# Moving loads between queues and skipping a round trip through memory in a fused retention / state-space layer on Trainium2

## The chip, the cores and the metric

The kernel runs on one NeuronCore of a Trainium2 chip. A core has five engines, each with an instruction queue that is worked off in order: TensorE (PE, matrix products), VectorE (DVE), ScalarE (ACT), GpSimd (POOL) and SyncE (SP, which only starts transfers). DMA transfers are started by an instruction on SP's, ACT's or POOL's queue. The metric is device time in microseconds (us); lower is better. Before the change the median of three runs is 2652.86 us (2648.1 to 2653.33).

## What is computed

One layer of a hybrid decoder in float32, on 1024 prompt tokens and 8 sample tokens (1032 columns, width 2048), with the same weights for both:

```python
def layer(x, pos, s_ret, s_re, s_im, ...):
    h = rmsnorm(x, g_pre)
    proj = h @ w_in                                   # 2048 x 10240
    q, k, v, za, ub, zb, ga, gb = jnp.split(proj, splits, axis=-1)
    ya, s_ret_new = retention(q, k, v, pos, s_ret)    # 8 heads, chunks of 128, normalized per head
    ya = (ya * jax.nn.silu(za)) @ w_pa
    yb, s_re_new, s_im_new = s5(ub, ...)              # ends in gelu and y * sigmoid(y @ w_glu + b_glu)
    yb = (yb * jax.nn.silu(zb)) @ w_pb
    merged = jax.nn.sigmoid(ga) * ya + jax.nn.sigmoid(gb) * yb
    out = merged @ w_out
    return x + rmsnorm(out, g_post), s_ret_new, s_re_new, s_im_new
```

## The kernel before

**Layout and products.** Tokens lie along the free axis, 1032 = 2 x 516 columns (`TOK` = 2 `HT`); features lie on the 128 partitions, so a 1024-wide activation is eight tiles. Each float32 product is three TensorE products of a high and a low part. `split` (L255) makes the two parts of a token tile: ACT casts a copy to the high part (L256) and DVE subtracts it from the source (L84, the line of every DVE addition, subtraction and product). Weights are split in the same way: L202 for plain products and L873 for the Strassen products.

**Stages, in order.** First `ub` and the S5 scan with the steps of `w_in`; retention runs as background work in the second half of `w_in` (about 1350 to 1822 us); then the gated linear unit of S5 (GLU, `linear(I["w_glu"], ...)`, 8 output tiles by 2 halves by 3 thirds of the tokens, to about 1913 us); then eight steps of `pa`, the first gated projection (`ya @ w_pa`), and eight of `pb` (`yb @ w_pb`) to about 2272 us; then `merged @ w_out` in two parts, first the rest of the tokens (392 columns), then the other 640.

**Strassen steps.** `w_in`, `pa` and `pb` go through 2 x 2 blocks of weights and token halves by a seven-product form. For one step, `fetch(s + 1)` starts the four weight loads (SP), `prep(g + 2)` makes weights two products ahead (DVE additions, ACT cast `whi`, DVE `wlo`), `product(g)` (L880) issues 48 plus 48 matmuls, and `evac_p` takes the result out of the accumulators; three accumulators rotate. The token operands are seven forms of the halves: u1 and v1 (halves of features 0 to 3 and 4 to 7), v2, and the four sums t1, t3, t2, t4 that `make_forms` builds. They sit in SBUF as split pairs found by `qslot("pa", n, i)` for product n and feature tile i; `order_q` is the list of the 28 pairs in the order of use.

**The GLU's background.** While the GLU's products run, `glu_forms` makes the forms of `pa`. `make_forms` loads the eight `ya_d` tiles into `fx` (POOL's queue), DVE builds the sums in place, and both halves of each form go to memory (`fa_d`). Then `stage` (L835) loads one half tile after another into eight `stg` buffers, 24 of the 28 within the GLU, and `unstage` splits them. The GLU's evacuation (`evac_glu`) is ACT's sigmoid (L1379), a DVE product, a store and the load of the next gate `zz<-zy_d`. Ahead of the GLU all left-over late work of the last `w_in` step is issued in one piece: `due` holds functions by product number (`at(g, f)`), `late_work(g)` issues them. In that last step they are the accumulation of partial sums (`u<-pt_d`), ACT's sigmoid on them (L972) and their stores to `sgb_d`.

**Gates and merging.** `load_z` (L1442) loads a gate half (`zz<-sga_d` in `pa`, `zz<-sgb_d` in `pb`) by POOL's queue. `gated` multiplies an evacuated result tile by it. In `pa` the product goes to `pap_d`. In `pb`, POOL adds `pap_d` onto the tile by an accumulating transfer (L1464), and four products later (`LAG`) stores the sum to `mg_d` (L1465). In the last step the second token half is added to a loaded `pap_d` half by DVE instead (L1445, L1460). `mg_load` (L1502) loads the 392 columns of merged tokens for the output stage by POOL, `mg_split` splits them (ACT, DVE).

**Retention.** `head(h)` is a generator; each `yield` is a step of background work given to the scheduler after a product. At its end come the normalization's statistics (DVE), the power -1/2 on POOL (L1135, L1136), `rsd` times a column and `nb` (DVE, L1137 to L1139), a `yield`, nine normalizations on ACT (L1142, L1143), a `yield`, and transposes on TensorE (L1149).

**What sets the order.** Background generators are advanced by `slot()` once a product. A scheduler then orders instructions by priority, and every engine's queue stays in that order.

Of the kernel before, what the change touches and what calls it, by code (L numbers as in the profile page):

```python
# [10 lines left out]
F32 = mybir.dt.float32  # L11
# [16 lines left out]
TA = 640  # L28
# [50 lines left out]
def emit(ctx, tc, I, O):  # L79
# [9 lines left out]
    def add(out, a, b, eng=None):  # L89
        return tt(out, a, b, ALU.add, eng)  # L90
# [164 lines left out]
    def split(dst, src):  # L255
        A.copy(dst[0], src)  # L256
        sub(dst[1], src, dst[0].bitcast(F32))
# [542 lines left out]
    def popen(name, side, bufs):  # L800
        st = ExitStack()
        return st, st.enter_context(tc.tile_pool(name=name, bufs=bufs, side=side))
# [14 lines left out]
    def qslot(kh, n, i):  # L817
        j = (2 * n + i // 2 + {0: 0, 1: -2, "pa": 4, "pb": 2}[kh]) % 16
        grp = 0 if kh in (0, 1) else kh
        if (grp, j) not in qtile:  # L820
            qtile[grp, j] = act.tile([128, 2, 2, HT], F32R, name=f"a{j}")
        return qtile[grp, j][:, i % 2, 0, :], qtile[grp, j][:, i % 2, 1, :]
# [3 lines left out]
    def stage(pool, kh, n, i, eng=P):  # L826
        r = stq[kh, n, i] = pool.tile([128, HT], F32, name="stg")
        if kh in (0, 1):
            src = fm_d[kh, n, i]
        else:  # L830
            y, F = (ya_d, fa_d) if kh == "pa" else (yb_d, fb_d)
            f = FORMS[n]
            src = {"u1": y[i], "v1": y[4 + i], "v2": y[4 + i], "t1": F[0, i], "t3": F[0, i], "t4": F[1, i], "t2": F[1, i]}[f]
            src = src[:, 0:HT] if f in ("u1", "v1", "t1", "t4") else src[:, HT:TOK]
        eng.dma_start(r, src)  # L835

    def unstage(kh, n, i):
        split(qslot(kh, n, i), stq.pop((kh, n, i)))
# [69 lines left out]
    def at(g, f):  # L908
        due.setdefault(g, []).append(f)
# [122 lines left out]
    def head(h):  # L1032
# [101 lines left out]
        V.tensor_scalar(rs[0:8, 8:9], mv[0:8, 8, 1:2], EPS, None, ALU.add)  # L1134
        P.tensor_tensor(rs[:, 0:8], rs[:, 0:8], mhalf, ALU.pow)  # L1135
        P.tensor_tensor(rs[0:8, 8:9], rs[0:8, 8:9], mhalf[0:8, 0:1], ALU.pow)  # L1136
        V.tensor_scalar(rs[:, 0:8], rs[:, 0:8], col[:, 2, h:h + 1], None, ALU.mult)  # L1137
        V.scalar_tensor_tensor(nb[:, 0:8], mv[:, 0:8, 0], -1.0, rs[:, 0:8], ALU.mult, ALU.mult)
        V.scalar_tensor_tensor(nb[0:8, 8:9], mv[0:8, 8, 0:1], -1.0, rs[0:8, 8:9], ALU.mult, ALU.mult)  # L1139
        yield  # L1140
        for n in range(8):
            A.activation(on[:, n], on[:, n], AF.Identity, scale=rs[:, n:n + 1], bias=nb[:, n:n + 1])  # L1142
        A.activation(ons, ons, AF.Identity, scale=rs[0:8, 8:9], bias=nb[0:8, 8:9])  # L1143
# [90 lines left out]
    def late_work(g):  # L1234
        with ExitStack() as after:
            for ins in anchor.values():
                after.enter_context(tc.issue_after(ins))
            for f in due.pop(g, ()):
                f()
# [4 lines left out]
    for s in range(2 * NP):  # L1244
# [41 lines left out]
        for n in range(7):  # L1286
# [26 lines left out]
                        at(g, lambda m=m: load_gy(6 + m))  # L1313
            late_work(g)
            slot()
    for g in sorted(due):
        late_work(g)
    gstack.close()


    bglu = const.tile([128, 8], F32, name="bglu")
# [9 lines left out]

    def stg_open(bufs):
        opened["stg"], opened["stgp"] = popen("stg3", "left", bufs)

    def make_forms(src, F):

        t = {}

        def ld(i):
            t[i] = [opened["fxp"].tile([128, TOK], F32, name="fx") for _ in range(2)]  # L1340
            for x, k in zip(t[i], (i, 4 + i)):
                P.dma_start(x, src[k])

        ld(0)
        ld(1)
        for _ in range(3):
            yield
        for i in range(4):
            u, v = t.pop(i)
            u1, u2, v1, v2 = u[:, 0:HT], u[:, HT:TOK], v[:, 0:HT], v[:, HT:TOK]  # L1350
            sub(u1, u1, u2)
            sub(u2, u2, v2)
            yield
            add(v2, v2, u1)
            sub(v1, v1, v2)
            P.dma_start(F[0, i], u)
            P.dma_start(F[1, i], v)
            yield
            if i < 2:
                yield  # L1360
                yield
                ld(i + 2)
                yield
        opened["fx"].close()
# [17 lines left out]
            load_zy(3 * m + t + 4)  # L1382
        return f

    def glu_forms():
        yield from make_forms(ya_d, fa_d)
        stg_open(8)
        for o in order_q[0:8]:
            stage(opened["stgp"], "pa", *o)
        for _ in range(3):  # L1390
            yield
        for z in range(16):
            unstage("pa", *order_q[z])
            stage(opened["stgp"], "pa", *order_q[z + 8])
            yield

    def tail_forms():
# [10 lines left out]
    for k in range(4):  # L1408
        load_zy(k)
    fx_open()  # L1410
    bg.append(glu_forms())
    S0 = 2 * NP
    lim[0] = 7 * len(steps)

# [23 lines left out]
    def load_z(s, name):  # L1438
        kind, p = steps[s]
        r, c = AT[name]  # L1440
        zq[name] = zz_tile()
        P.dma_start(zq[name], (sga_d if kind == "pa" else sgb_d)[2 * p + r, :, HT * c:HT * c + HT])  # L1442
        if s == len(steps) - 1 and c:
            zq[name, "p"] = zz_tile()
            P.dma_start(zq[name, "p"], pap_d[2 * p + r, :, HT * c:HT * c + HT])  # L1445

    def gated(g, name, t, ps=None):
        s = g // 7
        kind, p = steps[s]
        r, c = AT[name]  # L1450
        m, cols = 2 * p + r, slice(HT * c, HT * c + HT)
        z = zq.pop(name)
        if ps is None:
            mul(t, t, z)
        else:
            mul(two(t), ps, two(z))
        if kind == "pa":
            P.dma_start(pap_d[m, :, cols], t)
        elif (name, "p") in zq:
            add(t, t, zq.pop((name, "p")))  # L1460
            last_t[m] = t
            P.dma_start(mg_d[m, :, HT:TA], t[:, 0:TA - HT])
        else:
            P.dma_start(t, pap_d[m, :, cols], accum_op=ALU.add)  # L1464
            at(g + LAG, lambda: P.dma_start(mg_d[m, :, cols], t))  # L1465

    def evac_p(g, ps):
        n = g % 7
# [30 lines left out]

    def mg_load(m):  # L1500
        mgr[m] = mgp.tile([128, SW], F32, name="mga")
        P.dma_start(mgr[m], mg_d[m, :, TA:TOK])  # L1502

    def mg_split(m, src=None):
        mg_open(m)
        split((mg[m][0][:, TA:TOK], mg[m][1][:, TA:TOK]), mgr.pop(m) if src is None else src)
# [4 lines left out]
    for s in range(S0, len(steps)):  # L1511
        kind, p = steps[s]
        if s == S0 + 1:
            opened["stg"].close()
            fx_open()
            bg.append(make_forms(yb_d, fb_d))
        if s == S0 + 6:
            drain()
            stg_open(8)
        if s == S0 + 9:  # L1520
            opened["stg"].close()
            mgstack, mgp = popen("mgp", "left", 6)
        for n in range(7):
            g = 7 * s + n
            if n == 1:
                fetch(s + 1)
            prep(g + 2)
            evac_p(g, product(g))
            if n in (0, 2, 3, 4):
                at(g, lambda s=s, n=n: load_z(s, {0: "11", 2: "22", 3: "21", 4: "12"}[n]))  # L1530
            if s == S0 and n < 6:
                for _ in range((2, 1, 1, 1, 2, 1)[n]):
                    at(g, lambda o=order_q[pa_q[0]]: unstage("pa", *o))
                    if pa_q[0] + 8 < 28:
                        at(g, lambda o=order_q[pa_q[0] + 8]: stage(opened["stgp"], "pa", *o))
                    pa_q[0] += 1
            q = g - 7 * (S0 + 6)
            if 0 <= q < 4:
                for _ in range(2):
                    at(g, lambda o=order_q[nxt]: stage(opened["stgp"], "pb", *o))  # L1540
                    nxt += 1
            if 3 <= q < 20:
                for i in range(1 if q < 7 else 2):
                    if done_q < 28:
                        at(g, lambda o=order_q[done_q]: unstage("pb", *o))
                        done_q += 1
                        if nxt < 28:
                            at(g, lambda o=order_q[nxt]: stage(opened["stgp"], "pb", *o))
                            nxt += 1
            if s == SE - 1 and n in (1, 2, 3):  # L1550
                for m in (2 * n - 2, 2 * n - 1):
                    at(g, lambda m=m: mg_load(m))
            if s == SE - 1 and n in (5, 6):
                at(g, lambda m=n - 5: mg_split(m))
            if s == SE and n < 6:
                for m in (2 + 2 * n, 3 + 2 * n) if n < 5 else (13,):
                    at(g, lambda m=m: mg_split(m))
                for m in (6 + 2 * n, 7 + 2 * n) if n < 3 else ((13,) if n == 3 else (12,) if n == 4 else ()):
                    at(g, lambda m=m: mg_load(m))
            late_work(g)  # L1560
            slot()
    for m in (12, 15, 14):
        mg_split(m, last_t[m][:, TA - HT:HT] if m in last_t else None)
    for g in sorted(due):
        late_work(g)
    mgstack.close()
# [265 lines left out]
```

## Time and profile before

| what | before |
|---|---|
| median of the runs | 2652.86 us (2648.1 to 2653.33, 3 runs) |
| the profiled execution | 2650.8 us |
| its span | 2648.8 us |
| mean granted TensorE clock | 0.993 |
| gate loads `zz` from `sga_d`, `sgb_d` by POOL | 32 and 32, of 258 KB |
| loads of merged tokens `mga` by POOL | 14, of 196 KB |
| `ya_d` loads into `fx` | 8, of 516 KB |

An instruction row of the trace gives its start, its length, the engine (PEld is a weight load, POOLq a queue), the line, the operation, output and inputs, the size and, in brackets, how long the engine was idle before and what released it. In a wait row the numbers are the total, the count and the longest of the waits. Matmuls are pipelined and their ends are modelled.

Six windows of the span divide it by stage. The columns are window, length, busy time of PE, PEld, DVE, ACT and POOL (with counts), granted clock, DMA share, GB/s.

```profile
0.00:230.00 230.00, 224.53 (x1414) 222.24 (x1415) 135.94 (x204) 70.24 (x97) 28.66 (x67) 1.00 0.76 242
230.00:1350.00 1120.00, 1119.01 (x9277) 1111.62 (x9276) 918.91 (x2213) 377.91 (x667) 312.34 (x528) 1.00 0.54 152
1350.00:1822.00 472.00, 467.60 (x3955) 462.10 (x3954) 305.50 (x664) 212.52 (x395) 189.25 (x278) 1.00 0.79 215
1822.00:1913.00 91.00, 80.09 (x491) 79.35 (x490) 40.37 (x69) 28.45 (x52) 43.37 (x81) 0.94 0.89 300
1913.00:2272.00 359.00, 341.82 (x2780) 340.82 (x2779) 247.50 (x395) 109.60 (x191) 134.33 (x228) 0.98 0.74 221
2272.00:2648.00 376.00, 365.00 (x1744) 321.44 (x1744) 190.53 (x312) 154.74 (x278) 56.61 (x88) 0.99 0.61 194
```

TensorE is idle for about 11 us in the GLU and 17 us in `pa` and `pb`; the fourth and fifth rows are those stages. In the last row TensorE's last matmul begins at 2637.3 us.

### The profile page before, as it was taken

The numbers are of one execution on the slowest core, as the hardware profiler recorded it, in microseconds if no ns is written. First come the engines' busy times: TensorE is split into PE (matmuls) and PEld (weight loads), VectorE is DVE, ScalarE is ACT, GpSimd is POOL, SyncE is SP. The second block draws the span as 40 slices with busy tenths as digits, with TensorE's granted clock in tenths as the row PEclk, the third lists the DMA queues.
The fourth block names the chain that finished last, engine by engine and source line by source line (L and its number), as shares of the span: only waits on it lengthen the run. The fifth ranks groups of instructions, "written<-read, shape, count | busy, mean of one in ns | idle before, by whom it ended". The sixth has DMA issues, their size and how long they took to land. (4 is left out here: it accounts for less than half of the span.)

```text
span 2648.8 us, 51289 instructions
## 1 busy us (share of the span) xinstructions
PE 2598.1 (98%) x19652; PEld 2537.6 (96%) x19652; DVE 1838.8 (69%) x3853; ACT 953.5 (36%) x1679; POOL 764.6 (29%) x1268
## 2 busy tenths in 40 slices
PE   9999999999999999999999999999899999899998
PEld 8999999999999999999999999999899999898886
DVE  6655989889889867558877666665477865444555
ACT  6013233323333335442244444444332422343344
POOL 0103322222222223322244433333533434211111
PEclk9999999999999999999999999999999999899999
DMA  5886444443443457876688777779876767745666
GB/s 189 270 263 206 147 122 123 131 130 120 120 139 121 121 170 218 215 199 166 160 229 238 206 199 216 193 181 292 290 246 237 241 183 191 221 163 173 195 194 231
DMA packets 225525, 506.60 MB, mean 191 GB/s; under 512 B 32720, under 2 KB 53664, under 8 KB 225152
## 3 DMA queue, kind: packets, MB, share of 16 engines
q0 software_dynamic: 102672, 301.07, 40.5%
q1 hardware_dynamic: 103072, 179.57, 21.5%
q10 hardware_dynamic: 19536, 22.69, 2.8%
q8 instruction: 154, 2.52, 0.4%
q14 instruction: 91, 0.75, 0.1%
HBM read 345.20 MB, written 158.01 MB: 190 GB/s over the span
## 5 line engine op out<-in xcount | busy, mean ns | idle before, releaser
L892 PE MATMUL acc<-a,whi 128*128 128x258 f32 x9632 | 1565.7, 284 | 19.5 <-DVE u L84 16.1
L892 PEld LDWEIGHTS acc<-a,whi 128*128 128x128 f32 x9632 | 1328.4, 190 | 26.2 <-ACT whi L873 13.3
L892 PE MATMUL acc<-a,wlo 128*128 128x258 f32 x4816 | 970.4, 283 | 0.0
L892 PEld LDWEIGHTS acc<-a,wlo 128*128 128x128 f32 x4816 | 746.3, 190 | 0.0
L84 DVE TENSOR_TENSOR wlo<-wraw,whi 128x512 fp32r<-128x512 f32 x482 | 330.9, 687 | 238.7 <-ACT whi L202 141.9
L873 ACT CAST whi<-wraw 128x512 fp32r<-128x512 f32 x344 | 213.4, 620 | 617.5 <-PE acc L892 516.5
L873 ACT CAST whi<-wr 128x512 fp32r<-128x512 f32 x258 | 160.0, 620 | 517.8 <-PE acc L892 477.2
L209 PE MATMUL mm<-a,whi 128*128 128x384 f32 (+2 forms) x704 | 233.7, 333 | 8.3 <-ACT whi L202 5.4
L210 PE MATMUL mm<-a,whi 128*128 128x384 f32 (+2 forms) x704 | 233.5, 332 | 0.0
L211 PE MATMUL mm<-a,wlo 128*128 128x384 f32 (+2 forms) x704 | 232.3, 330 | 0.1
L84 DVE TENSOR_TENSOR wlo<-wr,whi 128x512 fp32r<-128x512 f32 x273 | 187.0, 685 | 53.1 <-ACT whi L873 43.0
L1730 PE MATMUL mm<-whi,a 128*128 128x512 f32 x512 | 171.1, 395 | 0.0
L202 ACT CAST whi<-wraw 128x512 fp32r<-128x512 f32 x138 | 85.5, 620 | 208.1 <-PE mm L210 104.6
L209 PEld LDWEIGHTS mm<-a,whi 128*128 128x128 f32 x704 | 133.0, 189 | 8.8 <-ACT whi L202 5.4
L211 PEld LDWEIGHTS mm<-a,wlo 128*128 128x128 f32 x704 | 133.7, 190 | 0.8 <-DVE wlo L84 0.6
L210 PEld LDWEIGHTS mm<-a,whi 128*128 128x128 f32 x704 | 133.5, 190 | 0.6 <-DVE a L363 0.6
L84 DVE TENSOR_TENSOR wraw<-wr 128x512 f32<-128x512 f32 x172 | 118.1, 687 | 5.9 <-DMA wr<-in_w_pa 3.7
L1730 PEld LDWEIGHTS mm<-whi,a 128*128 128x128 f32 x512 | 96.1, 188 | 22.8
L84 DVE TENSOR_TENSOR p<-acc,p 128x516 f32<-128x516 f32 x86 | 59.6, 693 | 72.9 <-PE acc L892 72.7
L84 DVE TENSOR_TENSOR wlo<-wx,whi 128x512 fp32r<-128x512 f32 x76 | 52.5, 691 | 76.0 <-ACT whi L202 75.7
L1730 PE MATMUL mm<-wlo,a 128*128 128x512 f32 x256 | 101.4, 396 | 0.0
L84 DVE TENSOR_TENSOR u<-acc,u 128x516 f32<-128x516 f32 x86 | 59.6, 693 | 59.9 <-PE acc L892 58.7
(369 smaller groups left out, 3483.7 us busy)
## 6 DMA issues: line engine op xcount, KB each, us to landing
wr<-in_w_in SPq DMA_DIRECT2D x280, 256.0 KB
pt_d<-u POOLq DMA_DIRECT2D x70, 258.0 KB, 3.1
u<-pt_d POOLq DMA_DIRECT2D x70, 258.0 KB, 5.3
wraw<-in_w_outB SPq DMA_DIRECT2D x66, 256.0 KB
stg<-fm_d POOLq DMA_DIRECT2D x44, 258.0 KB, 4.3
wx<-in_w_outB SPq DMA_DIRECT2D x43, 256.0 KB
wraw<-in_w_out SPq DMA_DIRECT2D x39, 256.0 KB
pt_d<-st POOLq DMA_DIRECT2D x35, 258.0 KB, 3.1
```

The lines of the kernel that those rows point to most:

```text
L84: return (eng or V).tensor_tensor(out, a, b, op)
L202: anchor["a"] = A.copy(hi, raw).ins
L209: T.matmul(ps, wh[:, i, :], xh[:, t0:t1], start=first, stop=False)
L210: T.matmul(ps, wh[:, i, :], xl[:, t0:t1], start=False, stop=False)
L211: anchor["p"] = T.matmul(ps, wl[:, i, :], xh[:, t0:t1], start=False, stop=last).ins
L873: anchor["a"] = A.copy(hi, f).ins
L892: anchor["p"] = T.matmul(ps[:, j, 0:258], a[:, i, :], b[:, 258 * j:258 * j + 258], start=first and i == 0 and a is wh and b is xh, stop=n ...
L1730: anchor["p"] = T.matmul(ps[c], a, b, start=k == 0 and a is xh and b is wh, stop=k == KD - 1 and a is xl).ins
```

## The change

The change has five parts.

1. In `head`, the `yield` moves up, so that DVE reads POOL's power one background step later.
2. The left-over late work of the last `w_in` step becomes a generator, `left_over`, that `both` advances together with `glu_forms` during the GLU.
3. The new `glu_forms` loads pairs of `ya_d` tiles into `fx` and splits the forms of products 0 to 3 straight from SBUF: u1, t2, v1 and t3. Only the halves t1 and t4 are stored to `fa_d`, and eight half tiles are staged for the rest of the GLU. That leaves out 16 staged loads and half of the stored bytes.
4. Gate loads, the two `pap_d` half loads of the last step and the merged-token loads are started by ACT's queue instead of POOL's.
5. In the last `pb` step, the addition of product "22" goes from DVE to POOL, the merged tokens 12 and 13 are split from the tiles that hold them in SBUF (two loads fewer), and 15 comes ahead of 14.

```diff
@@ head
         P.tensor_tensor(rs[0:8, 8:9], rs[0:8, 8:9], mhalf[0:8, 0:1], ALU.pow)
+        yield
         V.tensor_scalar(rs[:, 0:8], rs[:, 0:8], col[:, 2, h:h + 1], None, ALU.mult)
         V.scalar_tensor_tensor(nb[:, 0:8], mv[:, 0:8, 0], -1.0, rs[:, 0:8], ALU.mult, ALU.mult)
         V.scalar_tensor_tensor(nb[0:8, 8:9], mv[0:8, 8, 0:1], -1.0, rs[0:8, 8:9], ALU.mult, ALU.mult)
-        yield
@@ the end of the w_in steps
-    for g in sorted(due):
-        late_work(g)
     gstack.close()
+    def left_over():
+        for n in range(2, 8):
+            yield
+            for g in sorted(due):
+                if g - 14 * NP <= n - (n > 4) - 2:
+                    late_work(g)
@@ new
+    def glu_forms():
...
+        ld(0)
+        ld(1)
+        for _ in range(6):
+            yield
+        for i in range(4):
+            u, v = t.pop(i)
+            u1, u2, v1, v2 = u[:, 0:HT], u[:, HT:TOK], v[:, 0:HT], v[:, HT:TOK]
+            split(qslot("pa", 0, i), u1)
+            sub(u1, u1, u2)
+            yield
+            split(qslot("pa", 2, i), v1)
+            sub(u2, u2, v2)
+            yield
+            add(v2, v2, u1)
+            P.dma_start(fa_d[0, i, :, 0:HT], u1)
+            split(qslot("pa", 1, i), v2)
+            yield
+            sub(v1, v1, v2)
+            P.dma_start(fa_d[1, i, :, 0:HT], v1)
+            split(qslot("pa", 3, i), u2)
+            yield
+            if i < 2:
+                yield
+                yield
+                ld(i + 2)
+            yield
+        opened["fx"].close()
+        stg_open(8)
+        for o in order_q[16:24]:
+            stage(opened["stgp"], "pa", *o)
@@ load_z
-        P.dma_start(zq[name], (sga_d if kind == "pa" else sgb_d)[2 * p + r, :, HT * c:HT * c + HT])
+        A.dma_start(zq[name], (sga_d if kind == "pa" else sgb_d)[2 * p + r, :, HT * c:HT * c + HT])
...
-            P.dma_start(zq[name, "p"], pap_d[2 * p + r, :, HT * c:HT * c + HT])
+            A.dma_start(zq[name, "p"], pap_d[2 * p + r, :, HT * c:HT * c + HT])
@@ gated
-            add(t, t, zq.pop((name, "p")))
+            add(t, t, zq.pop((name, "p")), P if name == "22" else V)
...
+            if s == len(steps) - 2 and c:
+                last_t[m] = t
@@ mg_load
-        P.dma_start(mgr[m], mg_d[m, :, TA:TOK])
+        A.dma_start(mgr[m], mg_d[m, :, TA:TOK])
@@ the last pb step
-                for m in (2 + 2 * n, 3 + 2 * n) if n < 5 else (13,):
-                    at(g, lambda m=m: mg_split(m))
-                for m in (6 + 2 * n, 7 + 2 * n) if n < 3 else ((13,) if n == 3 else (12,) if n == 4 else ()):
+                for m in (2 + 2 * n, 3 + 2 * n):
+                    at(g, lambda m=m: mg_split(m, last_t[m][:, TA - HT:HT] if m in last_t else None))
+                for m in (6 + 2 * n, 7 + 2 * n) if n < 3 else ():
                     at(g, lambda m=m: mg_load(m))
```

How the instructions stand now is seen on three queues. First DVE at the end of one retention head, as a difference (- before, + now; `u` and `p` are evacuated result tiles, `wraw`, `wlo` weights):

```order
 L1134 TENSOR_SCALAR rsd<-mv 8x1
-L1137 TENSOR_SCALAR rsd<-rsd,col 128x8
-L1139 SCALAR_TENSOR_TENSOR nb<-mv,rsd 8x1
-L1138 SCALAR_TENSOR_TENSOR nb<-mv,rsd 128x8
 L84 TENSOR_TENSOR u_22229<-p_22164,acc 128x516
 L84 TENSOR_TENSOR wlo<-wraw,whi 128x512
-L84 TENSOR_TENSOR wraw<-wraw,wr 128x512
-L84 TENSOR_TENSOR wlo<-wr,whi 128x512
+L1138 TENSOR_SCALAR rsd<-rsd,col 128x8
+L1140 SCALAR_TENSOR_TENSOR nb<-mv,rsd 8x1
+L84 TENSOR_TENSOR wraw<-wraw,wr 128x512
+L1139 SCALAR_TENSOR_TENSOR nb<-mv,rsd 128x8
```

The evacuation `u` and one `wlo` now stand ahead of the reads of POOL's result, and the weight addition `wraw` stands between them and the large `nb`.

Then POOL's queue at the turn from `w_in` to the GLU. Before:

```order
L946 DMA p_22735<-pt_d 128x516
L973 DMA sgb_d<-u_22845 128x516
L1342 DMA fx<-ya_d 128x1032
L946 DMA u_22771<-pt_d 128x516
L973 DMA sgb_d<-p_22735 128x516
L1342 DMA fx<-ya_d 128x1032 x2
L973 DMA sgb_d<-u_22771 128x516
L1342 DMA fx<-ya_d 128x1032
```

The same place now (`pt_d` loads accumulate partial sums, `sgb_d` stores hold the gate):

```order
L946 DMA p_22735<-pt_d 128x516
L1346 DMA fx<-ya_d 128x1032 x2
L946 DMA u_22771<-pt_d 128x516
L1346 DMA fx<-ya_d 128x1032 x2
L973 DMA sgb_d<-u_22845 128x516
L973 DMA sgb_d<-p_22735 128x516
L973 DMA sgb_d<-u_22771 128x516
```

All four `fx` loads of the first two pairs moved ahead of the three `sgb_d` stores.

Last, POOL's queue through the second-to-last step of `pb`; middle steps read the same without the `mga` rows. Before:

```order
L1464 DMA u_27707<-pap_d 128x516
L1502 DMA mga<-mg_d 128x392
L1442 DMA zz<-sgb_d 128x516
L1465 DMA mg_d<-u_27707 128x516
L1464 DMA p_27591<-pap_d 128x516
L1502 DMA mga<-mg_d 128x392
L1445 DMA zz<-pap_d 128x516
L1464 DMA u_27634<-pap_d 128x516
L1502 DMA mga<-mg_d 128x392
L1465 DMA mg_d<-p_27591 128x516
L1442 DMA zz<-sgb_d 128x516
L1465 DMA mg_d<-u_27634 128x516
```

The same place now:

```order
L1511 DMA st<-pap_d 128x516
L1512 DMA mg_d<-st 128x516
L1511 DMA u_27675<-pap_d 128x516
L1512 DMA mg_d<-u_27675 128x516
L1511 DMA p_27559<-pap_d 128x516
L1511 DMA u_27602<-pap_d 128x516
L1512 DMA mg_d<-p_27559 128x516
L1512 DMA mg_d<-u_27602 128x516
```

The accumulating loads and their stores are left; the gate and merged-token loads are on ACT's queue.

More of the change, by code (lines that the diff above doesn't have):

```diff
@@ L1333, in stg_open, with ld @@
         opened["stg"], opened["stgp"] = popen("stg3", "left", bufs)
+    def glu_forms():
+        t = {}
+        def ld(i):
+            t[i] = [opened["fxp"].tile([128, TOK], F32, name="fx") for _ in range(2)]
+            for x, k in zip(t[i], (i, 4 + i)):
+                P.dma_start(x, ya_d[k])
+        ld(0)
[28 more added lines that the diff above has]
+            stage(opened["stgp"], "pa", *o)
     def make_forms(src, F):
@@ L1383, in evac_glu, with both @@
         return f
[L1385 to L1394, printed above, removed]
+    def both():
+        a, b = left_over(), glu_forms()
+        n = 0
+        while True:
+            live = False
+            for x in (a, b):
+                try:
+                    next(x)
+                    live = True
+                except StopIteration:
+                    pass
+            if not live:
+                return
             yield
@@ L1410, in emit @@
     fx_open()
-    bg.append(glu_forms())
+    bg.append(both())
     S0 = 2 * NP
@@ L1561, in emit @@
             slot()
-    for m in (12, 15, 14):
-        mg_split(m, last_t[m][:, TA - HT:HT] if m in last_t else None)
+    for m in (15, 14):
+        mg_split(m, last_t[m][:, TA - HT:HT])
     for g in sorted(due):
```

## The prediction

> **What bounds the kernel now.** I began with the page's busy times and then asked for the waits of TensorE alone.
>
> ```profile
> PE 2598.1 (98%) x19652; PEld 2537.6 (96%) x19652; DVE 1838.8 (69%) x3853; ACT 953.5 (36%) x1679; POOL 764.6 (29%) x1268
> ...
> PE acc L892 <- DVE u L84: 16.1, 12, 11.4
> PE acc L209 <- ACT p L1379: 10.2, 2, 9.2
> ...
> PE mm L209 <- DVE u L84: 2.9, 1, 2.9
> PE acc L892 <- ACT p L1471: 2.7, 1, 2.7
> ```
>
> TensorE is busy for 98% of the span and no matmul is added or removed, so the change can win only what TensorE loses. The waits (total, count, longest) are few: 10.2 us in the GLU, 2.7 us and one 0.73 us in the middle of `pb`, 11.4 and 2.9 us at its end, and eight short ones in retention. The second loss is the granted clock, which falls after each long stall. The windows below begin where TensorE restarts (columns: length, busy of PE, PEld, DVE, ACT, POOL, granted clock, DMA share, GB/s).
>
> ```profile
> 2198.60:2203.60 5.00, 4.81 (x28) 4.81 (x29) 4.09 (x7) 1.10 (x3) 0.35 (x1) 0.66 0.68 165
> 2261.20:2267.20 6.00, 6.00 (x29) 6.00 (x30) 3.77 (x7) 1.98 (x4) 2.60 (x5) 0.53 0.98 252
> 2272.60:2277.60 5.00, 4.95 (x19) 4.98 (x20) 3.36 (x6) 1.04 (x2) 1.10 (x2) 0.66 0.85 223
> 1879.20:1884.70 5.50, 5.44 (x17) 5.44 (x18) 5.50 (x11) 4.49 (x10) 4.27 (x8) 0.51 1.02 388
> ```
>
> Length times the missing clock is lost: 5.0 x 0.34 = 1.7, 6.0 x 0.47 = 2.8, 1.7 and 5.5 x 0.49 = 2.7 us. With these, the GLU stalls cost 10.2 + 2.7 = 12.9, the middle of `pb` 2.70 + 0.73 + 1.7 = 5.1, its end 11.4 + 2.9 + 2.8 + 1.7 = 18.8.
>
> **The GLU (parts 2 and 3).** The chain behind the long stall:
>
> ```profile
> 1871.97 2.12 POOL L835 DMA_DIRECT2D stg<-ya_d  x4 [0.95 <-DMA fa_d<-fx]
> ...
> 1876.84 1.89 ACT L256 CAST a<-stg 128x516 fp32r<-128x516 f32 x3 [12.83 <-DMA stg<-ya_d]
> ...
> 1878.63 0.57 ACT L1379 ACTIVATE p<-acc,bglu 128x384 f32<-128x384 f32 x1
> 1879.26 0.69 PE L209 MATMUL acc<-a,whi 128*128 128x384 f32 x1 [9.22 <-ACT p L1379]
> ```
>
> ACT sat 12.83 us in front of the cast of a staged tile; POOL had issued that load behind the last store of a form. The sigmoid, which frees TensorE's accumulator, is queued behind the casts. In the new order the casts read `fx`, and no staged load stands before a sigmoid until the last eight loads. On POOL the first two `fx` pairs now stand ahead of the last three `sgb_d` stores (the order shown above), where before single `fx` loads stood behind them. DVE and ACT do as many operations as before (16 splits, 16 form operations), and 16 loads and 8 x 258 KB of stores go away in a stretch where the DMA engines are 1.02 busy. What is late next is the first split, or the activation of a late tile in front of the first sigmoid; the second wait of the 10.2 us is of that kind:
>
> ```profile
> 1834.93 0.44 PE L209 MATMUL acc<-a,whi 128*128 128x384 f32 x1 [1.03 <-ACT p L1379]
> ...
> fx<-ya_d POOLq DMA_DIRECT2D x8, 516.0 KB, 6.6
> ```
>
> The `fx` loads take 6.6 us to land and the third and fourth pairs are issued only after two forms are done. Bounds: nothing left, or one landing of 6.6 us and the 2.7 us of slow clock left. I am near the lower end, since two pairs are loaded ahead: about 0.9 us remains, the size of the 1.03 wait. Term: -12.0 (-12.9 to -3.6).
>
> **The middle of `pb` (part 4).** The order of POOL's queue shown above (middle steps read alike without `mga`) explains these rows:
>
> ```profile
> 2182.25 0.70 DVE L84 TENSOR_TENSOR st<-acc,zz 128x516 f32<-128x516 f32 x1 [4.10 <-DMA zz<-sgb_d]
> ...
> 2194.75 0.56 POOL L1465 DMA_DIRECT2D mg_d<-p  x1 [4.80 <-DMA p<-pap_d]
> 2195.30 0.57 POOL L1442 DMA_DIRECT2D zz<-sgb_d  x1
> 2195.32 0.70 DVE L84 TENSOR_TENSOR p<-p,zz 128x516 f32<-128x516 f32 x1 [5.64 <-DMA zz<-sgb_d]
> ...
> 2198.15 0.59 ACT L1471 COPY p<-acc 128x516 f32<-128x516 f32 x1 [4.52 <-DMA mg_d<-p]
> ...
> 2184.30 0.73 PE L892 MATMUL acc<-a,whi 128*128 128x258 f32 x4 [0.73 <-DVE u L84]
> ...
> 2198.79 1.23 PE L892 MATMUL acc<-a,whi 128*128 128x258 f32 x4 [2.70 <-ACT p L1471]
> ```
>
> POOL waits in order for each accumulating transfer before it may store the sum, and the next gate load stands behind that wait: 4.80 us here. DVE then waits 5.64 us for a gate, the result tile is stored late, and ACT's copy into that tile 4.52 us later still, which TensorE sees as 2.70 us. On ACT's queue a gate load passes none of those waits. POOL's own chain is shorter by four issues a step, of 0.57 us in the row above. Both stalls should go: -5.1 (-5.1 to 0).
>
> The issues cost ACT time:
>
> ```profile
> 506.54 1.21 ACTq L715 DMA_DIRECT2D y_d<-a  x2
> ...
> 2187.23 0.62 ACT L873 CAST whi<-wraw 128x512 fp32r<-128x512 f32 x1 [3.25 <-PE acc L892]
> ```
>
> One issue holds ACT for 1.21 / 2 = 0.6 us. 78 of them are 47 us, 64 of them the gates of the 16 steps of `pa` and `pb`: 2.4 us a step. They hide in ACT's idle time: a weight cast here waits 3.25 us for TensorE to free its buffer. Cost 0, or 47 us if nothing hid them. I take 0, because the 3.25 of idle is five times an issue.
>
> The trace has no gate load on ACT's queue, only POOL's landing (`zz<-sgb_d`, 5.3 us in the row quoted with the rivals). The Trainium skill speaks against this part: the page "DMA: Bandwidth & Descriptors", section "Issuing engines are not separate DMA queues", says that transfers started by different engines share the same 16 DMA engines, so that more issuers save only the issuing time. The trace does not decide against it, but the 4.80 us in front of POOL's store are a wait in the issuer's order and not a busy DMA engine; taken strictly the rule would leave both `pb` terms in place (a rival below).
>
> **The end of `pb` (parts 4 and 5).**
>
> ```profile
> 2259.13 0.55 POOL L1465 DMA_DIRECT2D mg_d<-u  x1 [4.43 <-DMA u<-pap_d]
> 2259.32 0.52 ACT L256 CAST a<-mga 128x392 fp32r<-128x392 f32 x1 [4.10 <-DMA mga<-mg_d]
> ...
> 2261.19 1.20 PE L892 MATMUL acc<-a,whi 128*128 128x258 f32 x4 [11.40 <-DVE u L84]
> ...
> 2271.81 0.69 DVE L84 TENSOR_TENSOR u<-acc,u 128x516 f32<-128x516 f32 x1
> ...
> 2272.65 0.41 PE L209 MATMUL mm<-a,whi 128*128 128x392 f32 x1 [2.93 <-DVE u L84]
> ...
> 2301.30 1.07 POOL L84 TENSOR_TENSOR sp<-sp,st 128x392 f32<-128x392 f32 x1 [2.52 <-ACT st L1626]
> ```
>
> The merged tokens' loads (`mga`) stand on POOL behind the same accumulating transfers. ACT's cast of one waits for it, the weight cast behind it on ACT is late, and DVE's split and evacuations are late after both; TensorE stops for 11.4 us. Now loads for m = 6 to 11 are issued by ACT, whose sums were stored a whole step earlier, and m = 12, 13 need no load. The 2.93-us stall is another thing: the last evacuation stands on DVE behind splits and gate products and starts only at 2271.81. In the new order DVE still has two splits and a gate product ahead of it, so I leave 2.0 us of stall, its slow clock of 1.7 and 0.3 for an `mga` that lands late: 4.0 of 18.8. The "22" addition goes to POOL, where the nearest row is the last one of the fence: 1.07 us for 128x392, so about 1.4 by size, and the product it delays is needed first by the output stage's later loads; cost 0, at most 1.4. Term: -14.8 (-18.8 to 0).
>
> On the clock, the 2.70-us stall already brought 0.66, while no slow clock follows the 1.03-us one. The Trainium skill, "TensorE: Matmul & The Clock Gate", section "The HAM clock gate (the "warmup" mystery)", puts the fall after at least one free-running idle window of 3413 ns. The 2.70 us row differs from it; by the page the 2.0 us that I leave would keep the full clock, and the sum would be 1.7 lower.
>
> **Retention (part 1).**
>
> ```profile
> 1767.84 0.23 DVE L1137 TENSOR_SCALAR rsd<-rsd,col 128x8 f32<-128x8 f32 x1 [1.51 <-POOL rsd L1135]
> ...
> 1768.52 0.67 DVE L84 TENSOR_TENSOR u<-p,acc 128x516 f32<-128x516 f32 x1
> 1768.63 2.42 ACT L1142 ACTIVATE kT<-kT,nb,rsd 128x128 f32<-128x128 f32 x6 [1.75 <-DVE nb L1138]
> ...
> 1769.24 0.75 PE L892 MATMUL acc<-a,whi 128*128 128x258 f32 x4 [0.44 <-DVE u L84]
> ...
> 1769.83 0.69 DVE L84 TENSOR_TENSOR wraw<-wraw,wr 128x512 f32<-128x512 f32 x1
> ...
> 1772.23 1.04 PE L1149 MATMUL misc<-ident,kT 128*128 128x128 f32 x8
> ```
>
> DVE waits 1.51 us for POOL's power with the evacuation `u` behind it, and TensorE loses 0.44 us; eight heads make 3.5. In the new order `u` and `wlo` go first, so that goes. But `nb` now comes after the 0.69-us `wraw` addition: ACT's normalizations start about 0.7 us later, and their 2.42 us for six were done only just as TensorE's transposes began (1772.23). So up to 0.7 us a head comes back, 5.6 in all. Bounds -3.5 to +2.1 net if the wait goes, and +5.6 if it doesn't; I take **0**.
>
> **Sum.** 2650.8 (the profiled execution; its span is 2648.8) - 12.0 - 5.1 - 14.8 + 0 = 2618.9, rounded 2619. That execution is 2.1 below the median 2652.86 and inside the runs (2648.1 to 2653.3), so I forecast on its scale.
>
> **The rivals.** Two rows more:
>
> ```profile
> zz<-sgb_d POOLq DMA_DIRECT2D x32, 258.0 KB, 5.3
> ...
> mga<-mg_d POOLq DMA_DIRECT2D x14, 196.0 KB, 3.5
> ```
>
> (A) The GLU stall moves to the new splits waiting for `fx`: 6.6 + 2.7 = 9.3 remain instead of 0.9, 2627. For it: DMA share 1.02 there. Against: two pairs ahead.
> (B) The end of `pb` still waits for a merged token or for DVE: two landings of 3.5 and the slow clock of 1.7 more, 2628. For it: `mga` is a chain of transfers through memory; against: they are issued a step after their stores.
> (C) The queue does not matter, since a gate takes its 5.3 us to land on a loaded memory and comes late as before: 5.1 and 14.8 come back less some 3 us of issue time, 2636. The skill's rule named above would give this. Against: the 4.80 us wait of POOL ahead of the load.
> (D) Retention loses the 5.6: 2625.
> (E) Slower: ACT's own order becomes the bound. If the 78 issues at 0.6 us stand before weight casts that TensorE already waits for, 47 us are added to 2619: 2666. It decides as soon as ACT's lead (3.25 us) falls below the issue, or the issue itself holds for an earlier transfer's completion. Against: ACT is busy for 36% of the span.
>
> **How the numbers follow.** Forecast 0.56 (its own range 2607, with all four terms whole and the low run, to 2630), A 0.09, B 0.12, C 0.07, D 0.06, E 0.10, of which half is hidden enough to end within 0.2%. A measurement of this kernel tells about 0.2%, 5.3 us, from no change. All but E are faster by more. The range 2607 to 2637 takes in A to D and leaves E and the tails out. Faster 0.90, same 0.05, slower 0.05.
>
> **What would show it.** Right: no ACT wait on `stg<-ya_d` before 1880; the clock at 1.0 through the GLU; no DVE wait on `zz<-sgb_d`; the 11.4 gone, a stall of about 2 us before the first L209 of the output. Wrong: TensorE waits for ACT `whi` in `pa` or `pb` (E); DVE or ACT waits for `fx` (A); ACT L256 waits for `mga` (B); the L1149 transposes wait for ACT L1142 (D).

## The result and the profile after

The changed kernel takes 2633.43 us (median of 4 runs, 2632.4 to 2634.65) against 2651.95 us before (4 runs): ratio 0.9933, 95% interval 0.9915 to 0.995. The profiled execution took 2632.4 us with a span of 2630.6. The forecast was 2619 in a range of 2607 to 2637. The direction and the range held, but by the profiled executions (2650.8 before) only 18.4 of the 31.9 us came.

First the waits of TensorE in the changed kernel (total, count, longest):

```profile
PE mm L209 <- ACT whi L202: 9.4, 2, 5.2
PE mm L209 <- DVE u L84: 8.2, 1, 8.2
PE acc L209 <- ACT p L1423: 1.3, 1, 1.3
...
PE acc L209 <- ACT u L1423: 0.4, 1, 0.4
PE acc L892 <- DVE u L84: 0.4, 2, 0.2
```

The waits in `pb`'s products are gone (11.4, 2.7, 0.73), the GLU's fell from 10.2 to 1.3 and 0.4, and the retention heads' are no longer listed. Two waits at the output stage are new or larger: 8.2 where 2.9 stood, and half of the 9.4 (the other 5.2 is the kernel's start, as before).

Where the time went is read from the first and last starts of the matmuls of a stage, the two numbers around "to": `mm` L209 ends with the first part of the output, `acc` L209 is the GLU, L892 the Strassen steps. By these rows the GLU of the first kernel ends at 1926.6 us and not at about 1913, where the windows of the profile before divide it; its stalls lie ahead of both. Before the change:

```profile
L209 PE MATMUL mm<-a,whi x704: 279/339/687, 5.4 to 2411.5; 128*128 128x384 f32 x80, 128*128 128x392 f32 x64, 128*128 128x264 f32 x32
L209 PE MATMUL acc<-a,whi x192: 278/333/686, 1822.4 to 1926.6; 128*128 128x384 f32 x128, 128*128 128x264 f32 x64
...
L892 PE MATMUL acc<-a,whi x9632: 277/283/584, 240.5 to 2269.2; 128*128 128x258 f32 x197
```

The same rows of the changed kernel:

```profile
L209 PE MATMUL mm<-a,whi x704: 282/339/695, 5.2 to 2392.6; 128*128 128x384 f32 x80, 128*128 128x392 f32 x64, 128*128 128x264 f32 x32
L209 PE MATMUL acc<-a,whi x192: 283/333/448, 1822.1 to 1914.5; 128*128 128x384 f32 x128, 128*128 128x264 f32 x64
...
L892 PE MATMUL acc<-a,whi x9632: 277/283/389, 240.8 to 2237.4; 128*128 128x258 f32 x197
```

| stretch | before | after | won |
|---|---|---|---|
| start to the GLU | 1822.4 | 1822.1 | 0.3 |
| GLU | 104.2 | 92.4 | 11.8 |
| GLU's end to the last `pb` product | 342.6 | 322.9 | 19.7 |
| last `pb` product to the last L209 | 142.3 | 155.2 | -12.9 |
| from there to the end of the span | 237.3 | 238.0 | -0.7 |

So nearly the whole forecast had been won by the last product of `pb` (31.8 us), and 12.9 were given back behind it. The timeline of the changed kernel shows how (start, length, instruction, idle time before and its releaser):

```profile
2234.12 0.56 POOL L1512 DMA_DIRECT2D mg_d<-u  x1 [6.83 <-DMA u<-pap_d]
...
2235.23 1.24 POOL L1511 DMA_DIRECT2D u<-pap_d  x1
...
2241.36 0.52 ACT L256 CAST a<-u 128x392 fp32r<-128x392 f32 x1 [6.71 <-DMA u<-pap_d]
2241.91 0.57 DVE L84 TENSOR_TENSOR a<-u,a 128x392 fp32r<-128x392 f32 x1 [6.04 <-ACT a L256]
...
2246.12 0.67 PE L209 MATMUL mm<-a,whi 128*128 128x392 f32 x1 [8.21 <-DVE u L84]
...
2260.92 1.16 POOL L1649 DMA_DIRECT2D z<-mg_d  x2
...
2266.82 0.72 ACT L256 CAST a<-z 128x640 fp32r<-128x640 f32 x1 [5.81 <-DMA z<-mg_d]
...
2270.06 0.69 PE L209 MATMUL mm<-a,whi 128*128 128x392 f32 x1 [4.17 <-ACT whi L202]
```

The tile of feature block 12 lies in SBUF, but `pap_d` must be added to it first, and POOL starts that accumulating load only at 2235.23, at the end of the following step. ACT stands 6.71 us at its cast, DVE 6.04 behind it, with the last evacuations queued behind both. Then POOL, still late, starts the loads `z<-mg_d` at 2260.92; ACT waits 5.81 us at the cast of the first, with weight casts behind it, and TensorE stops a second time. Both stalls are followed by a halved clock (columns as in the prediction):

```profile
2246.10:2251.10 5.00, 4.98 (x15) 5.00 (x16) 1.26 (x3) 0.73 (x2) 2.33 (x3) 0.50 0.68 228
2270.00:2275.00 5.00, 4.94 (x14) 4.50 (x15) 2.99 (x6) 3.27 (x7) 1.96 (x3) 0.50 0.80 239
```

8.2 + 4.2 and twice 5.0 x 0.50 = 2.5 for the slow clock, 17.4 us in all, stand at the end of `pb` now, against 18.8 before.

### The profile page after: what moved, and what is told of

The parts are those of the page before. It is cut to its first block, busy times and chain, and to the rows that moved or that the text cites. A ratio compares the mean times of both kernels' runs of the same rounds, so it can differ in the third digit from the quotient of the medians.

```text
span 2630.6 us, 51277 instructions
## 1 busy us (share of the span) xinstructions
PE 2596.9 (99%) x19652; PEld 2532.8 (96%) x19652; DVE 1840.2 (70%) x3852; ACT 956.6 (36%) x1679; POOL 716.5 (27%) x1173
## 5 line engine op out<-in xcount | busy, mean ns | idle before, releaser
L892 PE MATMUL acc<-a,whi 128*128 128x258 f32 x9632 | 1562.3, 284 | 1.0 <-ACT whi L873 0.6
L892 PEld LDWEIGHTS acc<-a,whi 128*128 128x128 f32 x9632 | 1326.6, 190 | 5.4 <-issue 2.4
L892 PE MATMUL acc<-a,wlo 128*128 128x258 f32 x4816 | 969.1, 282 | 0.0
L892 PEld LDWEIGHTS acc<-a,wlo 128*128 128x128 f32 x4816 | 744.7, 189 | 0.0
L873 ACT CAST whi<-wraw 128x512 fp32r<-128x512 f32 x344 | 213.8, 622 | 618.5 <-PE acc L892 508.0
L873 ACT CAST whi<-wr 128x512 fp32r<-128x512 f32 x258 | 160.3, 621 | 515.6 <-PE acc L892 442.0
L209 PE MATMUL mm<-a,whi 128*128 128x384 f32 (+2 forms) x704 | 235.0, 335 | 17.6 <-ACT whi L202 9.4
L209 PEld LDWEIGHTS mm<-a,whi 128*128 128x128 f32 x704 | 133.8, 190 | 18.7 <-ACT whi L202 9.9
L84 DVE TENSOR_TENSOR u<-acc,p 128x516 f32<-128x516 f32 x86 | 59.6, 693 | 62.5 <-PE acc L892 62.1
```

The lines of the kernel that those rows point to most:

```text
L84: return (eng or V).tensor_tensor(out, a, b, op)
L209: T.matmul(ps, wh[:, i, :], xh[:, t0:t1], start=first, stop=False)
L873: anchor["a"] = A.copy(hi, f).ins
L892: anchor["p"] = T.matmul(ps[:, j, 0:258], a[:, i, :], b[:, 258 * j:258 * j + 258], start=first and i == 0 and a is wh and b is xh, stop=n ...
```

## The experiments

Every time below is a median with the lowest and highest run, followed for most by the ratio to the first kernel and its 95% interval. The first kernel's own median lay between 2648.0 and 2652.0 us in the sessions of these runs, so a difference of less than about 4 us between two experiments is not shown by the medians alone.

**Is POOL's chain late, or are the transfers slow?** POOL's in-order work on each `pb` tile is an accumulating load, a wait for it, and a store. Of the eight loads `st<-pap_d`, one in every step, here are the first and the last in the changed kernel, and the gate product of DVE that the last one follows:

```profile
2086.16 0.88 POOL L1511 DMA_DIRECT2D st<-pap_d  x1 [4.92 <-DVE st L84]
...
2226.43 0.70 DVE L84 TENSOR_TENSOR st<-acc,zz 128x516 f32<-128x516 f32 x1
...
2242.13 0.93 POOL L1511 DMA_DIRECT2D st<-pap_d  x1
```

Seven steps take 156.0 us, 22.3 each, and the later loads don't wait for DVE any more: POOL is behind. Its first load starts 1.0 us after DVE's product (2085.16), the last 15.7 us after it. The chain was late before the change too:

```profile
2098.18 0.88 POOL L1464 DMA_DIRECT2D st<-pap_d  x1 [4.38 <-DVE st L84]
...
2249.67 0.69 DVE L84 TENSOR_TENSOR st<-acc,zz 128x516 f32<-128x516 f32 x1
...
2261.78 0.93 POOL L1464 DMA_DIRECT2D st<-pap_d  x1
```

That is 23.4 us a step, and the last load starts 12.1 us after its product; in between the lag had reached 19.5 us (product at 2157.68, load at 2177.20), and at the next step the gates behind POOL's waits stopped DVE for 4.10 us. The first experiment takes the waits for the stores out of that chain.

```diff
-            at(g + LAG, lambda: P.dma_start(mg_d[m, :, cols], t))
+            at(g + LAG, lambda: nc.sync.dma_start(mg_d[m, :, cols], t))
```

> The changed kernel with one edit: in pb the stores of the sums to mg_d are started by SP's queue, so that POOL no longer waits in order for each accumulating load before it starts the next. Theory 1 (POOL's chain of accumulate, wait, store takes 22.3 us a step against TensorE's 20.2, lags, and its debt is paid at the end of pb): accumulations start when their product is there, the 8.2 us stall before the output's first matmul falls below 3 us, the 4.2 us stall 24 us later goes, and with their slow clock the time falls from about 2632.5 to 2617 to 2622. Theory 2 (the transfers themselves are slow because the DMA engines are full there, whoever issues them): the stalls stay, 2630 to 2634. Against both: SP waits for sums and holds back weight loads; then TensorE waits in the middle of pb and the time rises.

It took 2618.36 us (2617.17 to 2619.34), ratio to before 0.9881 (0.9866 to 0.9895). The same loads, first and last of eight, and the stall that is left:

```profile
2087.30 0.88 POOL L1511 DMA_DIRECT2D st<-pap_d  x1 [4.93 <-DVE st L84]
...
2228.32 0.85 POOL L1511 DMA_DIRECT2D st<-pap_d  x1 [6.59 <-DVE st L84]
...
2242.46 0.67 PE L209 MATMUL mm<-a,whi 128*128 128x392 f32 x1 [3.17 <-DVE u L84]
```

Now seven steps take 141.0 us, 20.15 each: TensorE's own pace (322.9 us for 16 steps of `pa` and `pb`), with each of these loads 1.0 us behind its product. POOL waits for DVE 6.59, 6.11, 2.04 and 2.02 us in one such step (from 2167.82 on), 16.8 in all. The four store issues that left it, of 0.56 us, free only 2.2 us of that, so nearly all of the time won on POOL was waiting. Whether the issues alone would have sufficed, at 22.3 - 2.2 = 20.1 us a step, is not tested. The 8.2-us stall is 3.2, the 4.2-us one is gone. The transfers themselves did not get shorter throughout: from issue to landing `u<-pap_d` takes a median of 5.4 us here and 6.3 in the changed kernel, `p<-pap_d` 5.3 and 5.8, but `st<-pap_d` 6.2 and 5.4. SP now takes the waits (total, count, longest):

```profile
SPq L1512 <- DMA u<-pap_d: 53.2, 14, 6.3
SPq L1512 <- DMA st<-pap_d: 38.9, 7, 6.8
```

No product of TensorE waited longer for a weight because of them. Theory 1 holds.

The second experiment takes two of the last accumulations out of POOL's chain.

```diff
-        if s == len(steps) - 1 and c:
+        if s >= len(steps) - 2 and c:
             zq[name, "p"] = zz_tile()
...
-            add(t, t, zq.pop((name, "p")), P if name == "22" else V)
+            add(t, t, zq.pop((name, "p")), P if name == "22" and s == len(steps) - 1 else V)
```

> The changed kernel with one edit: the second-to-last pb step adds its second token half as the last step does (pap_d loaded by ACT's queue into a gate buffer, addition on DVE), in place of two accumulating loads on POOL. The bytes moved are nearly the same. Theory 1 (POOL's lagging chain): two of the last accumulations and their waits, some 12 us, leave the chain, and the splits of tokens 12 and 13 wait for DVE alone: the 8.2 us stall falls below 3, the 4.2 us stall goes or halves, 2617 to 2623. Theory 2 (full DMA engines): no gain, 2630 to 2634.

2623.79 us (2621.45 to 2626.82), 0.9903 (0.9887 to 0.992), just above the expected 2617 to 2623. The first stall is 1.10 us; the second is still 3.52, more than hoped: POOL goes through the remaining accumulations one by one as before.

**Is only the place of the split wrong?**

```diff
-            if s == SE and n < 6:
+            if s == SE and n < 5:
...
-    for m in (15, 14):
+    for m in (12, 13, 15, 14):
```

> The changed kernel with one edit: the splits of merged tokens 12 and 13 are issued behind the last product instead of at its sixth product. Theory 3 (only their place ahead of ACT's weight casts and DVE's last evacuations is wrong): the 8.2 us stall falls to 2 or 3 us and the time to 2621 to 2626; the 4.2 us stall stays. Theory 1 (POOL's chain is late): the tiles themselves are late, so a stall moves to the twelfth feature tile of the first output product; of the 8.2 us at most half is won, and the 4.2 us stall stays: 2628 to 2632.

2631.93 us (2629.32 to 2635.6). No gain is shown: in the order that resulted the cast of block 12 still stood ahead of the last evacuations, and ACT waited there for the same sum.

```profile
2244.81 0.52 ACT L256 CAST a<-u 128x392 fp32r<-128x392 f32 x1 [10.58 <-DMA u<-pap_d]
...
2249.57 0.67 PE L209 MATMUL mm<-a,whi 128*128 128x392 f32 x1 [10.51 <-DVE u L84]
```

So theory 3 found no support, though a place truly behind the evacuations wasn't reached.

**Do both remedies treat one cause?** The two edits above together:

> The changed kernel with both edits, the mg_d stores of pb on SP's queue and the addition by DVE in the second-to-last step. If both act on one cause, POOL's chain, they do not add: 2615 to 2619, near the first alone (2618.4). If they acted on two causes their gains (15.1 and 9.6 us) would add: below 2612.

2616.45 us (2615.09 to 2616.92), 0.9867 (0.9852 to 0.9881). The gains of 15.1 and 9.6 us don't add. By itself that proves less than the expectation says, since their sum of 24.7 us is more than the 17.4 that stand at the end of `pb`: it shows that both edits remove the same stalls. That the cause is POOL's chain rests on its time per step and its lag above. This is the lowest median found (its interval overlaps that of the first edit alone), and one stall of 1.58 us is left at the output's first matmul.

**The addition on POOL (part 5).**

```diff
-            add(t, t, zq.pop((name, "p")), P if name == "22" else V)
+            add(t, t, zq.pop((name, "p")))
```

> The changed kernel with one piece of part 5 undone: the addition of product 22 in the last step is DVE's again. The prediction gave its place on POOL a cost of 0 to 1.4 us. If POOL's chain sets the late merged-token loads, 1.3 us leave that chain and the 4.2 us stall shrinks by about as much: 2630 to 2633. Rival: on DVE the addition waits for the pap_d half in front of the split and the last evacuations, and the first stall grows by 1 to 3 us: 2634 to 2637.

2627.12 us (2624.82 to 2629.61), 0.9916 (0.9899 to 0.9933): 6.3 us better than the changed kernel by the medians (4.5 by the ratios), more than the first theory gave; the rival is refuted. The four runs form two pairs, near 2625 and near 2629.5, and the profiled execution is of the faster one. The first stall fell from 8.2 to 6.3 and the second almost went:

```profile
2243.50 0.66 PE L209 MATMUL mm<-a,whi 128*128 128x392 f32 x1 [6.34 <-DVE u L84]
2264.36 0.45 PE L209 MATMUL mm<-a,whi 128*128 128x392 f32 x1 [0.77 <-ACT whi L202]
```

In the changed kernel that addition stood on POOL behind the wait for a store and ahead of the last accumulation:

```profile
2248.46 0.56 POOL L1512 DMA_DIRECT2D mg_d<-st  x1 [5.40 <-DMA st<-pap_d]
2249.03 1.30 POOL L84 TENSOR_TENSOR u<-u,zz 128x516 f32<-128x516 f32 x1
...
2251.19 0.92 POOL L1511 DMA_DIRECT2D p<-pap_d  x1
```

The gate product of this sum was done by DVE at 2235.9, so the tile lay there for 13 us, and ACT's split of it (2250.37) waits 6.95 us for POOL. Not all of the gain is the edit's, though. POOL's order is the same in both kernels up to this addition, and yet in the profiled execution of this run block 12's accumulating load starts at 2228.76 and not at 2235.23, and ACT's cast of its sum at 2238.14 and not at 2241.36. That 3.2 us is more than the first stall lost, so the fall of the first stall is not shown to be the edit's. The load `z<-mg_d` behind the second stall starts 5.3 us earlier (2255.61); the last `st<-pap_d`, ahead of the addition, was already 3.2 earlier.

A test of whether that place makes the price, with the chain on pace (the edits of `sp_store` and this one):

> The kernel sp_store (mg_d stores of pb on SP's queue) with the addition of product 22 on DVE again. In the changed kernel this edit won 6.3 us. If it won them because the addition stood in POOL's late chain (behind the wait for a store, ahead of the last accumulation and of the merged-token loads), it wins next to nothing once the chain keeps pace: 2616 to 2619, against 2618.4 for sp_store. Rival: POOL's addition is slow in itself for the output stage; then another 4 to 6 us go: 2612 to 2614.

2619.53 us (2617.74 to 2620.63), 0.989 (0.9873 to 0.9906), no gain over `sp_store` alone (2618.36). No cost of the addition is seen where POOL keeps pace.

**The queue of the gates (part 4 undone).**

```diff
-        A.dma_start(zq[name], (sga_d if kind == "pa" else sgb_d)[2 * p + r, :, HT * c:HT * c + HT])
+        P.dma_start(zq[name], (sga_d if kind == "pa" else sgb_d)[2 * p + r, :, HT * c:HT * c + HT])
...
-            A.dma_start(zq[name, "p"], pap_d[2 * p + r, :, HT * c:HT * c + HT])
+            P.dma_start(zq[name, "p"], pap_d[2 * p + r, :, HT * c:HT * c + HT])
...
-        A.dma_start(mgr[m], mg_d[m, :, TA:TOK])
+        P.dma_start(mgr[m], mg_d[m, :, TA:TOK])
```

> The changed kernel with part 4 undone: gate loads, pap_d half loads and merged-token loads are started by POOL again. Theory 1 (gates behind POOL's chain of accumulations pace TensorE, so the chain cannot lag far): the stalls in the middle of pb come back (5.1 us with their slow clock before), and the end of pb keeps a stall of 6 us or more: 2636 to 2642. Rival C of the prediction (the queue does not matter but for the issue time): 2632 to 2635.

2639.91 us (2635.28 to 2643.07), 0.9955 (0.9937 to 0.9972). The old stalls stand where they stood:

```profile
2185.81 1.23 PE L892 MATMUL acc<-a,whi 128*128 128x258 f32 x4 [2.68 <-ACT p L1520]
...
2250.12 1.20 PE L892 MATMUL acc<-a,whi 128*128 128x258 f32 x4 [12.76 <-DVE u L84]
```

So the queue matters, as the change assumed, and rival C falls; the three kinds of loads went back together, so their shares are not separated. POOL's chain is late here as well, 23.6 us a step (`st<-pap_d` from 2086.21 to 2251.40), and the last load is 13.2 us behind its product. With the gates on POOL the late chain stops TensorE inside `pb` already: 2.7 and 0.5 us in the middle of `pb`, 12.8 at its last product, then 3.5 and 2.7 at the output. With the gates on ACT TensorE runs ahead and pays only at the output, 8.2 and 4.2.

**The GLU's two parts.** Part 2 undone (the left-over work issued in one piece):

```diff
+    for g in sorted(due):
+        late_work(g)
     gstack.close()
```

> The changed kernel with part 2 undone: the left-over late work is issued in one piece ahead of the GLU; part 3 stays. If part 3 carries the GLU's gain, as the prediction's chain said (staged loads behind form stores), the time stays at 2631 to 2635 and no stall over 2 us stands in the GLU. Rival: with the fx loads behind all the left-over stores again, ACT's splits wait for fx, and a stall of 5 us or more with slow clock returns: 2638 to 2642.

2635.43 us (2634.92 to 2639.74), 0.9944 (0.9926 to 0.9962). Part 3 undone (the old `glu_forms`, advanced by `both`):

```diff
-        for o in order_q[16:24]:
-            stage(opened["stgp"], "pa", *o)
+        yield from make_forms(ya_d, fa_d)
+        stg_open(8)
+        for o in order_q[0:8]:
+            stage(opened["stgp"], "pa", *o)
...
+        for z in range(16):
+            unstage("pa", *order_q[z])
+            stage(opened["stgp"], "pa", *order_q[z + 8])
+            yield
```

> The changed kernel with part 3 undone: forms go through memory and 24 half tiles are staged in the GLU, as before; part 2 stays. The prediction's chain for the 9.2 us stall (ACT's cast of a staged tile ahead of the sigmoid) should be back at nearly its size, with the slow clock behind it: 2642 to 2647. Rival: part 2 alone brings the loads early enough: 2632 to 2636.

2638.5 us (2635.25 to 2645.3, 5 runs), 0.9954 (0.9938 to 0.997). By the medians the two cost 2.0 and 5.1 us against the changed kernel, and neither expectation held cleanly. The GLU's extent and its longest stall, of the first kernel and then of the second:

```profile
L209 PE MATMUL acc<-a,whi x192: 282/333/650, 1822.1 to 1918.1; 128*128 128x384 f32 x128, 128*128 128x264 f32 x64
...
1837.66 0.65 PE L209 MATMUL acc<-a,whi 128*128 128x384 f32 x1 [4.08 <-ACT p L1425]
```

```profile
L209 PE MATMUL acc<-a,whi x192: 283/333/690, 1826.6 to 1926.6; 128*128 128x384 f32 x128, 128*128 128x264 f32 x64
...
1879.17 0.69 PE L209 MATMUL acc<-a,whi 128*128 128x384 f32 x1 [5.44 <-ACT p L1384]
```

From 104.2 us before, part 3 alone brings 96.0, part 2 alone 100.0, both 92.4. Part 3 wins 8.2 and part 2 4.2. Without part 2 ACT waits in turn for a left-over sum, an `fx` load, a second sum and a second `fx` load (4.14, 2.36, 1.12 and 1.58 us), and the sigmoid stands behind them; without part 3 the staged tile is back at 5.4 us in place of 9.2. In the second kernel the GLU began 4.5 us later, with 3.1 of them at a wait early in retention that is 0.4 or less elsewhere; its cause wasn't sought, and the extents leave it out.

**Retention (part 1).**

```diff
-        yield
         V.tensor_scalar(rs[:, 0:8], rs[:, 0:8], col[:, 2, h:h + 1], None, ALU.mult)
...
+        yield
```

> The changed kernel with part 1 undone: the yield in the retention head stands behind nb again. My prediction's value was 0 for this part. If it holds, the eight waits of 0.44 us for the evacuation come back, the eight transposes of a head take 1.04 us again instead of 1.79, and the time is within 1 us of the changed kernel. Rival: part 1 won its 3.5 us and the give-back is not real; then this kernel is 3 to 5 us slower than the changed one.

2633.29 us (2628.79 to 2636.14), 0.9936 (0.9921 to 0.995), within 0.2 us of the changed kernel. The waits of this kernel, and its transposes as a group over 1350 to 1822 us (busy time, mean ns | idle before):

```profile
PE acc L892 <- DVE u L84: 4.3, 11, 0.5
...
L1149 PE MATMUL misc<-ident,kT 128*128 128x128 f32 x64 | 8.3, 272 | 0.0
```

The same group in the changed kernel, and one head of it:

```profile
L1149 PE MATMUL misc<-ident,kT 128*128 128x128 f32 x64 | 14.1, 296 | 0.9
...
1771.12 1.79 PE L1149 MATMUL misc<-ident,kT 128*128 128x128 f32 x8
```

Undoing brings back the waits for `u`, 4.3 us, and shortens the transposes by as much or more: eight took 1.04 us and take 1.79 in the changed kernel, since they now follow ACT's normalizations one by one. As the ends of matmuls are modelled, that wait hardly shows as idle time of PE; it shows on the weight loads of the same group, which were idle for 5.4 us, in 23 waits, for ACT's normalizations. Taken together the two effects nearly cancel: the GLU's first matmul starts at 1822.1 us in the changed kernel and at 1823.4 with part 1 undone. The next experiment puts a further `yield` ahead of the transposes, on top of `sp_add2`, to remove that wait:

> The kernel sp_add2 with one more edit: in the retention head a further yield stands between ACT's normalizations and TensorE's transposes, so that the transposes come one product later. If the 0.75 us that each group of eight transposes gained in length is what part 1 gave back, it now goes, and 4 to 6 us are won: 2611 to 2614. Rival: the lengthening is only how the profile shows a group of small matmuls; then nothing changes, 2615 to 2618.

2618.64 us (2616.79 to 2619.02), 0.9879 (0.9865 to 0.9894): no gain, and just above both expected ranges. The transposes got shorter (10.3 us in the group), but other steps of retention now pressed (two more waits are of 1.0 and 0.8 us):

```profile
PE misc L1150 <- ACT kT L1142: 1.9, 1, 1.9
...
PE misc L1113 <- DVE ktS L84: 1.4, 1, 1.4
```

## Why the prediction was right or wrong

- **The bound.** Right: no matmul changed, and all that moved was TensorE's waits and the clock behind them.
- **The GLU, -12.0.** Measured -11.8, and the remainder is of the kind that I named (1.3 and 0.4 us in front of a sigmoid). The share of part 2 (4.2 alone) was larger than the reasoning gave it.
- **The middle of `pb`, -5.1.** Right: both stalls went, and putting the gates back on POOL brought one of 2.68 us back. Up to the last product the terms said 5.1 + 11.4 + 2.8 = 19.3 us; 19.7 were measured.
- **The issues on ACT, 0.** Right: the one wait for ACT's `whi` L873 is 0.6 us, as before. Rival E didn't occur. A gate load's row on ACT's queue shows 0.33 us, about half of the 0.6 that the prediction took.
- **The end of `pb`, -14.8.** This is the step that failed: 17.4 us stand there and not 4.0, which is -1.4. I wrote that blocks 12 and 13 "need no load" and took their tiles for ready. Their sums hang on accumulating loads in POOL's queue. The prediction had all the numbers for the check that it didn't make: POOL's waits of 4.43 and 4.80 us for one load and the 0.56 of the store behind it, four times a step, come to 20 or 21 us without the load's own issue, and TensorE's step is 20.2. I noted that POOL's chain got shorter and did not ask whether it was short enough: it went from 23.4 to 22.3 us a step. Once gates no longer made TensorE wait for it, the chain fell behind by about 2 us a step, and the sum came due at the first reader of its results. Rival B was near in place (the end of `pb` waits), not in mechanism. With the waits taken out of POOL's queue the rest of this term held: a stall of 3.17 us and a clock of 0.70 behind it are left, 4.7 us where 4.0 were forecast, and the kernel takes 2618.36.
- **The range.** That 2633 lies in it is in part luck. The forecast's own range ended at 2630; the stretch to 2637 was there for rival C, and C did not occur.
- **The "22" addition, 0 to 1.4.** Too small: undoing it won 6.3 us by the medians, of which not all is the edit's. I priced it by its duration (1.30 us against the estimate of 1.4) and took the output stage's later loads for the first readers of its result. The first reader is ACT's split, which waited 6.95 us; the addition was dear because of what it stands behind and ahead of on a late queue.
- **Retention, 0.** Right, and by the mechanism given: the wait for POOL's power no longer holds back the evacuation, and later normalizations lengthened the transposes by 0.75 us a head (0.7 was the estimate).

By the profiled executions: 13.4 of the 13.5 us between forecast and result lie in the end of `pb`.

## What to carry to other kernels

An engine's queue that makes others wait also paces them; when the wait is taken away, compare the queue's own time per step (here 22.3 us) with the pace that it must now keep (20.2), and look for the first reader of what it makes. A chain "load, wait, store" in one queue cost its latency each time here, and handing only the waiting store to another queue was worth 15.1 us, more than all the moved loads (6.5 us lost when they went back). A small operation on a late queue is to be priced by the queue and not by its length.

## What the runs showed of the hardware

The clock. The lengths of TensorE's stalls rest on modelled ends of matmuls. Stalls of 1.10 and 1.58 us at the output's first matmul (the kernels `add2` and `sp_add2`) were followed by a granted clock of 1.00 over the next 5 us, one of 2.65 us (`poolq`, at the second stall) by 0.70, and those of 4.17 and 8.21 by 0.50. By the Trainium skill, "TensorE: Matmul & The Clock Gate", section "The HAM clock gate (the "warmup" mystery)", at least one idle window of 3413 ns comes first; the stalls of 2.65 and 2.70 us with a lower clock behind them are shorter than that. Here are the windows of `sp_add2` and of `poolq`:

```profile
2239.50:2244.50 5.00, 4.95 (x28) 4.98 (x29) 3.53 (x6) 2.67 (x5) 0.58 (x1) 1.00 0.81 190
```

```profile
2282.70:2287.70 5.00, 4.62 (x17) 4.29 (x18) 3.81 (x6) 3.25 (x7) 2.11 (x3) 0.70 0.82 238
```
